# Gate product of a decoder block: weights' split ahead of the gates in each step, the last sum of weights added from SBUF, fewer products on GpSimd

## The chip, the cores and the metric

The kernel runs on one core of a Trainium2 chip, in one launch. The metric is device time in microseconds (us) of that core; the kernel before takes 863.55 us (median of three executions, 863.21 to 864.05). All data are float32. Matrix products are made with three float32r passes: each operand is cut into a rounded part ("hi", by ScalarE) and the rest ("lo", by VectorE), and hi·hi, hi·lo and lo·hi are summed.

## The reference, cut to what matters

Sequence 512, width 1024. A gated convolution and an mLSTM branch are merged into the residual stream `x`; then comes the end of the block, where the change lies:

```python
x = x + jnp.einsum('bsd,de->bse', merged, w_o[l])
gate = jax.nn.sigmoid(jnp.einsum('bsd,de->bse', rmsnorm(x, g_ple[l]), w_ple_gate[l]))
x = x + gate * jnp.einsum('bsp,pd->bsd', p[l], w_ple[l])
return rmsnorm(x, g_final)
```

`p·w_ple` was made early and waits in DRAM (`ple_d`). What is left at the end of the kernel is the gate's product (512 x 1024 by 1024 x 1024), the sigmoid, the gated addition, the sum of squares of each row, and the last scaling.

## The kernel before, in words

The gate's product is done by a Strassen scheme of seven products of half size. Its left operands are 256 rows by 512 (sums of quarters of the transposed `x`), its right operands 512 x 512 quarters of `w_ple_gate` or sums of them. g11, g21, g22, g12 are the four quarters, loaded in that order into four raw buffers. In the order of the program:

| product | left | weights | PSUM bank | what follows each half |
|---|---|---|---|---|
| 0 | g_a11 | g11 | acc | copy out (`snap`) |
| 1 | g_s1 | g11+g12 | cc | copy out |
| 2 | g_a12 | g21 | bb | gate of rows 2 or 3, first half (`g1`) |
| 3 | g_s2 | g11+g12+g22 | acc | copy out |
| 4 | g_s4 | g22 | cc | gate of rows 2 or 3, second half (`g3`) |
| 5 | g_s3 | g12+g22 | acc | gate of rows 0 or 1, second half (`g5`) |
| 6 | g_a22 | all four | acc | gate of rows 0 and 1, first half (`gated`) |

Product n uses operand n. The list `operands` holds, for each, the raw buffer that it is split from and the sums that are made once it has been split: operand 0 is split from g11, which then gets g12 added; operand 1 from the same buffer, which then gets g22; operand 2 from g21, after which g12 gets g22; operand 3 again from g11's buffer (three quarters by now), which then gets g21 and so holds all four for operand 6; operand 4 from g22, operand 5 from g12. The sums are DMAs of GpSimd's queue that add a quarter from DRAM into the raw buffer (line 179), 512 KB for each half.

Each product has two halves `i` of 128 rows, each of 12 matmuls of 128x512 (four `kt` by three passes, L227 to L229); a "row" below is one of the four groups of 128 rows of `x`. Splitting one half of an operand (`split_half`) is one ScalarE instruction (hi, L172, 128x1024) and one VectorE instruction (lo, L173); half 0 holds kt 0 and 1, half 1 kt 2 and 3. Operands 1 to 4 go through two sets of shared buffers (`whi`, `wlo`); the others have tiles of their own: operand 0 `wearly`, 5 `wlate`, 6 `wlast`.

Order is set by hand: no scheduler moves anything on TensorE, VectorE, ScalarE or GpSimd, and each engine runs its instructions strictly in the order in which the program issues them. After each half product the program calls `step`, which calls `tick`. A tick first starts the work that follows the last half product (`fresh`), then splits one half of an operand from the queue `pieces`, then goes on with older work (`active`). `next_operand` empties `pieces` before a product begins and queues the next operand.

After products: `gate` adds two sums (VectorE, L1348) and takes the sigmoid (ScalarE, L1349). `embed` multiplies with `ple` (VectorE, L1295) and adds to `x`, either on VectorE (L1299) or as an adding DMA from SBUF to SBUF by GpSimd's queue (L1297); before, rows 2 and 3 use the DMA. `squares` is a ScalarE instruction (L1302); `add_base`, `power`, `final_scale` are tiny VectorE and GpSimd instructions for the row's factor. `final` writes half a row of output: either VectorE multiplies `x` by the factor and by `g_final` (L1326, stored by SP's queue), or ScalarE scales a product `xg = x * g_final` that GpSimd made earlier (`weigh`, L1334; L1324, stored by ScalarE's queue). Before, GpSimd makes four such products and ScalarE writes four of the eight half rows.

Of the kernel before, what the change touches and what calls it, by code (L numbers as in the profile page):

```python
# [14 lines left out]
P = 128  # L15
# [14 lines left out]
HC = 4  # L30
# [6 lines left out]
def hybrid_block(ctx, tc, x, p, g_mix, w_in, conv_w, conv_b, w_a_out, b_gates, g_head,  # L37
# [87 lines left out]
    for n in range(2):  # L125
# [4 lines left out]
    operands.extend([(g11, [(g11, g12, None)]), (g11, [(g11, g22, None)]), (g21, [(g12, g22, None)]),  # L130
                     (g11, [(g11, g21, None)]), (g22, []), (g12, []), (g11, [])])
# [9 lines left out]
    state = {"raw": 0, "split": 0, "use": 0}  # L141
# [28 lines left out]
    def split_half(i, h, e_lo=None):  # L170
# [1158 lines left out]
    def weigh(t, n):  # L1329

        if not xg:
            u = ep.tile([P, 4, CW], F32, name="xg", tag="fx", align_bytes=256)
            xg.update({key: u[:, i, :] for i, key in enumerate(((3, 0), (3, 1), (0, 1), (1, 1)))})
        pool.tensor_tensor(xg[(t, n)], xr[:, t, half[n]], gfin[:, half[n]], ALU.mult)  # L1334
# [16 lines left out]
    def g1(i):  # L1351
# [9 lines left out]
        if t == 3:  # L1361
            weigh(t, 0)

    def g3(i):
# [4 lines left out]
        embed(c, t, half[1], True)  # L1369
        yield  # L1370
        yield
        yield
        squares(t, half[1], 1)
        power(t, 1)
        if t == 3:
            weigh(t, 1)

    def g5(i):
# [4 lines left out]
        weigh(i, 1)  # L1383
        add_base(i, 0)

    def cut_one():
        if pieces:
            split_half(*pieces.popleft())

    for left, banks, tag, post in ((g_a11, acc, order[0], snap(sn, "s", acc)), (g_s1, cc, order[1], snap(sv, "v", cc)),  # L1390
# [4 lines left out]
        if left is g_s2:  # L1395
            i = early + 5
            own[i] = [glp.tile([P, HC, CW], F32R, name="wlate", tag=f"gl{v}", align_bytes=256) for v in (0, 2)]
            pieces.extend((i, h) for h in range(2))
            u = hp.tile([P, 2, HC, CW], F32R, name="wlast", tag="vv", align_bytes=256)
            last = [u[:, v] for v in range(2)]  # L1400
        for i in range(2):
# [6 lines left out]
            if left is g_s2:  # L1408
# [3 lines left out]
        if left is g_s2:  # L1412
# [69 lines left out]
```

## Time and profile before

| | |
|---|---|
| median of three executions | 863.55 us |
| profiled execution, its own time | 864.67 us |
| its span, first to last instruction | 862.9 us |
| TensorE busy | 844.0 us (98%) |
| VectorE busy | 643.0 us (75%) |
| ScalarE busy | 501.7 us (58%) |
| GpSimd busy | 230.8 us (27%) |
| mean granted TensorE clock | 0.992 |

Times in a trace are us from the span's start. A matmul's row lasts longer than the distance to the next, since matmuls are pipelined; the same holds, less strongly, for VectorE and ScalarE. In brackets behind a row stands how long the engine was idle before it and what ended that. GpSimd's busy time holds its DMA issues.

### The profile page before, as it was taken

How to read it: one execution, taken by the hardware profiler on the slowest of the kernel's cores; microseconds unless marked ns; L12 is line 12 of the kernel's file. 1: busy time of each engine (PE TensorE's matmuls, PEld its weight loads, DVE VectorE, ACT ScalarE, POOL GpSimd, SP SyncE). 2: the span in 40 equal slices, each digit the busy share in tenths (PEclk: the TensorE clock that was granted, in tenths of full speed). 3: DMA queues.
4: the chain of work that ended last, by engine and by line, in shares of the span. 5: the costliest groups of instructions: out<-in, count | busy, mean ns of one | idle time of the engine just before them, and what ended most of it. 6: DMA issues, size and time to landing. Idle time of an engine off the chain costs nothing.

```text
span 862.9 us, 12184 instructions
## 1 busy us (share of the span) xinstructions
PE 844.0 (98%) x4634; PEld 734.1 (85%) x4634; DVE 643.0 (75%) x835; ACT 501.7 (58%) x737; POOL 230.8 (27%) x233
## 2 busy tenths in 40 slices
PE   8999999999999999999999999999999999999983
PEld 7888888888899988888788999999988888888863
DVE  5786767975877675788676879788876789955765
ACT  7467655667755566565776554645452366535654
POOL 5103222203225331320232434242410122111423
PEclk9999999999999999999999999999999999999996
DMA  9749669779968997896997799898995697665844
GB/s 313 263 135 186 156 135 219 183 280 239 257 130 195 247 214 171 188 221 218 246 240 179 188 192 180 177 186 203 169 403 209 100 236 177 206 232 146 196 74 122
DMA packets 102890, 172.82 MB, mean 200 GB/s; under 512 B 5612, under 2 KB 46112, under 8 KB 101552
## 3 DMA queue, kind: packets, MB, share of 16 engines
q0 software_dynamic: 41424, 76.10, 46.3%
q1 hardware_dynamic: 58256, 90.45, 31.6%
q10 hardware_dynamic: 3152, 5.51, 1.8%
q8 instruction: 36, 0.59, 0.3%
q14 instruction: 22, 0.18, 0.1%
HBM read 154.21 MB, written 16.78 MB: 198 GB/s over the span
## 4 chain that ended last, share of the span: by engine, by line
PE 90%; DVE 4%; ACT 3%; issue 1%; DMA 1%; SPq 0%; ACTq 0%; POOL 0%; DVEq 0%
PE mm L227 27%; PE mm L228 27%; PE mm L229 27%; PE pv L227 1%; PE pv L229 1%; PE pv L228 1%; DMA wraw<-in_w_ple 1%; PE pty L809 1%; PE sc L229 1%; PE sc L228 1%; PE sc L227 1%; ACT whi L172 1%; DVE wlo L173 0%; DVE gs L1295 0%; DVE gs L1348 0%
## 5 line engine op out<-in xcount | busy, mean ns | idle before, releaser
L173 DVE TENSOR_TENSOR wlo<-wraw,whi 128x1024 fp32r<-128x1024 f32 x238 | 297.3, 1251 | 120.5 <-ACT whi L172 119.8
L172 ACT ACTIVATE whi<-wraw 128x1024 fp32r<-128x1024 f32 x240 | 250.8, 1054 | 105.9 <-PE mm L229 43.7
L179 POOL DMA_DIRECT2D wraw<-in_w_in x112 | 136.8, 1421 | 317.4 <-DVE wlo L173 236.6
L343 ACT ACTIVATE s<-mm 128x512 f32<-128x512 f32 x84 | 50.2, 597 | 99.1 <-PE mm L229 97.9
L227 PE MATMUL mm<-whi,hs 128*128 128x512 f32 x256 | 99.9, 390 | 0.0
L228 PE MATMUL mm<-wlo,hs 128*128 128x512 f32 x256 | 99.9, 390 | 0.0
L229 PE MATMUL mm<-whi,hs 128*128 128x512 f32 x256 | 99.7, 390 | 0.0
L227 PE MATMUL mm<-hn_hi,whi 128*128 128x256 f32 (+1 forms) x304 | 93.4, 307 | 0.0
L229 PE MATMUL mm<-hn_hi,wlo 128*128 128x256 f32 (+1 forms) x304 | 93.0, 306 | 0.0
L228 PE MATMUL mm<-hn_lo,whi 128*128 128x256 f32 (+1 forms) x304 | 92.9, 306 | 0.0
L227 PE MATMUL mm<-hs,whi 128*128 128x256 f32 x320 | 90.9, 284 | 0.0
L229 PE MATMUL mm<-hs,wlo 128*128 128x256 f32 x320 | 90.6, 283 | 0.0
L228 PE MATMUL mm<-hs,whi 128*128 128x256 f32 x320 | 90.6, 283 | 0.0
L227 PE MATMUL mm<-whi,hn_hi 128*128 128x512 f32 x192 | 75.4, 393 | 0.0
L228 PE MATMUL mm<-wlo,hn_hi 128*128 128x512 f32 x192 | 75.0, 391 | 0.0
L229 PE MATMUL mm<-whi,hn_lo 128*128 128x512 f32 x192 | 74.8, 389 | 0.0
L228 PEld LDWEIGHTS mm<-hs,whi 128*128 128x128 f32 x320 | 61.4, 192 | 0.0
L227 PEld LDWEIGHTS mm<-hs,whi 128*128 128x128 f32 x320 | 61.4, 192 | 0.0
L229 PEld LDWEIGHTS mm<-hs,wlo 128*128 128x128 f32 x320 | 61.4, 192 | 0.0
L229 PEld LDWEIGHTS mm<-hn_hi,wlo 128*128 128x128 f32 x304 | 58.1, 191 | 2.5
L228 PEld LDWEIGHTS mm<-hn_lo,whi 128*128 128x128 f32 x304 | 58.1, 191 | 2.4
L227 PEld LDWEIGHTS mm<-hn_hi,whi 128*128 128x128 f32 x304 | 58.1, 191 | 2.4
(362 smaller groups left out, 1718.6 us busy)
## 6 DMA issues: line engine op xcount, KB each, us to landing
wraw<-in_w_in SPq DMA_DIRECT2D x32, 1024.0 KB, 5.4
wraw<-in_w_in POOLq DMA_DIRECT2D x52, 512.0 KB, 7.9
wraw<-in_w_in SPq DMA_DIRECT2D x48, 512.0 KB, 5.2
wraw<-in_w_in POOLq DMA_DIRECT2D x60, 256.0 KB, 6.0
wraw<-in_w_b_out SPq DMA_DIRECT2D x7, 1024.0 KB, 6.2
wraw<-in_w_b_out POOLq DMA_DIRECT2D x12, 512.0 KB, 6.5
yt_d<-yc POOLq DMA_DIRECT2D x4, 1024.0 KB, 4.9
wraw<-in_w_a_out SPq DMA_DIRECT2D x4, 1024.0 KB, 5.8
```

What stands on the lines that cost most here:

```text
L172: act.activation(hi, t, AF.Copy)
L173: (e_lo or dve).tensor_tensor(lo, t, hi.bitcast(F32), ALU.subtract)
L179: nc.gpsimd.dma_start(raws[to][:, ks, cs], src[:, ks, :], accum_op=ALU.add)
L227: pe.matmul(ps, lhsT=a[0], rhs=b[0], start=first, stop=False, **kw)
L228: pe.matmul(ps, lhsT=a[0], rhs=b[1], start=False, stop=False, **kw)
L229: pe.matmul(ps, lhsT=a[1], rhs=b[0], start=False, stop=last, **kw)
L343: act.activation(to[i], src, AF.Copy, scale=scale)
L809: pe.transpose(pts[v][:, t * P:(t + 1) * P], y[:, t, v * P:(v + 1) * P], ident)
```

## The change

1. In the gate's product a tick splits a half operand first and starts the gates afterwards (`weights_first`).
2. Operand 5 (`wlate`) is split in the steps of product 1 (before: product 3), and operand 6 (`wlast`) in the steps of product 2 (before: product 4). Product 2's steps now split operand 3's two halves and `wlast`'s two. Their tiles change places to what is free at that time.
3. The sum of all four quarters is made in g21 instead of g11: when operand 2 has been split from g21, a DMA of GpSimd's queue adds the raw g11 (three quarters by then) from SBUF into g21. That replaces the two DRAM additions behind operand 3.
4. `embed` of rows 2 and 3, second half, adds on VectorE instead of by DMA.
5. GpSimd makes two products `xg` instead of four; row 3's output is made by VectorE and stored by SP. The order of the last instructions is changed accordingly.

```diff
-    operands.extend([(g11, [(g11, g12, None)]), (g11, [(g11, g22, None)]), (g21, [(g12, g22, None)]),
-                     (g11, [(g11, g21, None)]), (g22, []), (g12, []), (g11, [])])
+    operands.extend([(g11, [(g11, g12, None)]), (g11, [(g11, g22, None)]), (g21, [(g12, g22, None), (g21, g11, "here")]),
+                     (g11, []), (g22, []), (g12, []), (g21, [])])
...
+            if eng == "here":
+                nc.gpsimd.dma_start(raws[to][:, ks, :], raws[c][:, ks, :], accum_op=ALU.add)
+                continue
...
     def tick():
+        if state["weights_first"]:
+            cut_one()
         new = [g for g in fresh if not next(g, True)]
         fresh.clear()
-        if pieces:
-            split_half(*pieces.popleft())
+        if not state["weights_first"]:
+            cut_one()
         active[:] = [g for g in active if not next(g, True)] + new
...
     def g3(i):
         t = 2 + i
         c = sn[i]
         gate(c, cc[i], t, ner)
         yield
-        embed(c, t, half[1], True)
-        yield
-        yield
-        yield
+        embed(c, t, half[1])
         squares(t, half[1], 1)
+        yield
         power(t, 1)
-        if t == 3:
-            weigh(t, 1)
...
-        if left is g_s2:
-            i = early + 5
-            own[i] = [glp.tile([P, HC, CW], F32R, name="wlate", tag=f"gl{v}", align_bytes=256) for v in (0, 2)]
-            pieces.extend((i, h) for h in range(2))
-            u = hp.tile([P, 2, HC, CW], F32R, name="wlast", tag="vv", align_bytes=256)
-            last = [u[:, v] for v in range(2)]
+        if left is g_s1:
+            u = hp.tile([P, 2, HC, CW], F32R, name="wlate", tag="vv", align_bytes=256)
+            place(early + 5, u[:, 0], u[:, 1])
+        if left is g_a12:
+            place(early + 6, *[glp.tile([P, HC, CW], F32R, name="wlast", tag=f"gl{v}", align_bytes=256) for v in (0, 2)])
...
             step(post(i))
-            if left is g_s2:
+            if left is g_a12:
                 cut_one()
...
+    final(2, 1)
     gated(1, 1)
     squares(0, q[1], 2)
     power(0, 2)
-    final(2, 1)
+    final_scale(3)
+    final(3, 0)
     squares(1, q[1], 2)
     power(1, 2)
-    final_scale(3)
-    final(3, 0, True)
-    final(3, 1, True)
+    final(3, 1)
     final_scale(0)
     final(0, 1, True)
     final(0, 0)
```

Three places show what this does to the order. In these rows the raw buffers are wraw_7091 (g11), wraw_7170 (g21), wraw_7278 (g22) and wraw_7342 (g12), and the lines of the changed kernel are 9 higher from L200 on.

First, GpSimd's queue around products 0 and 1, before:

```order
L179 DMA wraw_7091<-in_w_ple_gate 128x2x512 x4
L179 DMA wraw_7342<-in_w_ple_gate 128x2x512 x2
L1165 DMA ple<-ple_d 128x1024 x4
L1257 TENSOR_TENSOR etmp_7118<-etmp_7117,mhalf 128x4
L179 DMA wraw_7091<-in_w_ple_gate 128x2x512 x2
```

and in the changed kernel:

```order
L182 DMA wraw_7091<-in_w_ple_gate 128x2x512 x4
L182 DMA wraw_7342<-in_w_ple_gate 128x2x512
L177 DMA wraw_7170<-wraw_7091 128x1024
L182 DMA wraw_7342<-in_w_ple_gate 128x2x512
L177 DMA wraw_7170<-wraw_7091 128x1024
L1174 DMA ple<-ple_d 128x1024 x4
L1266 TENSOR_TENSOR etmp_7118<-etmp_7117,mhalf 128x4
```

The second addition into g12 now stands behind the first addition from SBUF, and the loads of `ple` and the power of L1257 (now L1266) behind the second one.

Second, ScalarE from the first copy of product 0's sums to the operand of product 4, before (gf: quarter of the transposed `x`; glb: left operands g_a12 and g_s4; gs: copies and gates):

```order
L1342 ACTIVATE gs<-mm 128x512
L1195 ACTIVATE gf_7533<-ptk,prm 128x256 x2
L1195 ACTIVATE gf_7534<-ptk,prm 128x256 x2
L234 ACTIVATE glb<-gf_7533 128x512
L234 ACTIVATE glb<-gf_7534 128x512
L1342 ACTIVATE gs<-mm 128x512 x2
L172 ACTIVATE whi_7613<-wraw_7091 128x1024
L234 ACTIVATE glb<-fx 128x1024
L1349 ACTIVATE gs<-gs,er 128x512
L172 ACTIVATE whi_7635<-wraw_7091 128x1024
L1349 ACTIVATE gs<-gs,er 128x512
L172 ACTIVATE whi_7657<-wraw_7278 128x1024
```

and the later part of the same stretch in the changed kernel:

```order
L172 ACTIVATE wlate<-wraw_7342 128x1024
L1351 ACTIVATE gs<-mm 128x512
L172 ACTIVATE whi_7620<-wraw_7091 128x1024
L1351 ACTIVATE gs<-mm 128x512
L243 ACTIVATE glb<-fx 128x1024
L172 ACTIVATE whi_7628<-wraw_7091 128x1024
L172 ACTIVATE wlast<-wraw_7170 128x1024
L1358 ACTIVATE gs<-gs,er 128x512
L172 ACTIVATE wlast<-wraw_7170 128x1024
L172 ACTIVATE whi_7663<-wraw_7278 128x1024
L1358 ACTIVATE gs<-gs,er 128x512
L172 ACTIVATE whi_7683<-wraw_7278 128x1024
```

The second half of `wlate` stands ahead of operand 3's first half, both halves of `wlast` ahead of operand 4's first half, and a gate's sigmoid between each pair. (The first half of `wlate` stands one copy earlier, ahead of L1195's rows.)

Third, VectorE over the same products, before:

```order
L1236 TENSOR_TENSOR fx<-fx,gf_7534 128x512
L173 TENSOR_TENSOR wlo_7614<-wraw_7091,whi_7613 128x1024
L235 TENSOR_TENSOR glb<-fx,glb 128x1024
L1348 TENSOR_TENSOR gs<-gs,mmb 128x512
L173 TENSOR_TENSOR wlo_7636<-wraw_7091,whi_7635 128x1024
L1348 TENSOR_TENSOR gs<-gs,mmb 128x512
L173 TENSOR_TENSOR wlo_7658<-wraw_7278,whi_7657 128x1024
L1295 TENSOR_TENSOR gs<-gs,ple 128x512
L173 TENSOR_TENSOR wlo_7664<-wraw_7278,whi_7663 128x1024
```

and in the changed kernel:

```order
L1245 TENSOR_TENSOR fx<-fx,gf_7536 128x512
L173 TENSOR_TENSOR wlo_7621<-wraw_7091,whi_7620 128x1024
L244 TENSOR_TENSOR glb<-fx,glb 128x1024
L173 TENSOR_TENSOR wlo_7629<-wraw_7091,whi_7628 128x1024
L173 TENSOR_TENSOR wlast<-wraw_7170,wlast 128x1024
L1357 TENSOR_TENSOR gs<-gs,mmb 128x512
L173 TENSOR_TENSOR wlast<-wraw_7170,wlast 128x1024
L173 TENSOR_TENSOR wlo_7664<-wraw_7278,whi_7663 128x1024
L1357 TENSOR_TENSOR gs<-gs,mmb 128x512
L1304 TENSOR_TENSOR gs<-gs,ple 128x512
L173 TENSOR_TENSOR wlo_7684<-wraw_7278,whi_7683 128x1024
```

Operand 3's second half (wlo_7629) now precedes the first gate instead of following it, and the two halves of `wlast` precede operand 4's (wlo_7664, wlo_7684).

More of the change, by code (lines that the diff above doesn't have):

```diff
@@ L140, in hybrid_block @@
                 last_use[c] = i
-    state = {"raw": 0, "split": 0, "use": 0}
+    state = {"raw": 0, "split": 0, "use": 0, "weights_first": False}
     raws, splits, pieces, active, fresh = {}, {}, deque(), [], []
@@ L189, in queue_split @@
         i = state["split"]
-        if i in own:
+        while i in own:
             i += 1
@@ L194, in queue_split, with cut_one @@
             pieces.extend((i, h) for h in range(2))
+    def cut_one():
+        if pieces:
+            split_half(*pieces.popleft())
     def next_operand(follow=True):
@@ L1327, in final, with weigh @@
         (nc.scalar if on_act else nc.sync).dma_start(out[0, t * P:(t + 1) * P, half[n]], y)
-    def weigh(t, n):
+    def weigh(t):
         if not xg:
-            u = ep.tile([P, 4, CW], F32, name="xg", tag="fx", align_bytes=256)
-            xg.update({key: u[:, i, :] for i, key in enumerate(((3, 0), (3, 1), (0, 1), (1, 1)))})
-        pool.tensor_tensor(xg[(t, n)], xr[:, t, half[n]], gfin[:, half[n]], ALU.mult)
+            u = ep.tile([P, 2, CW], F32, name="xg", tag="fx", align_bytes=256)
+            xg.update({(t, 1): u[:, t, :] for t in range(2)})
+        pool.tensor_tensor(xg[(t, 1)], xr[:, t, half[1]], gfin[:, half[1]], ALU.mult)
     acc, bb, cc, sn, sv = ([None, None] for _ in range(5))
@@ L1360, in g1 @@
         add_base(t, 0)
-        if t == 3:
-            weigh(t, 0)
     def g3(i):
@@ L1368, in g3 @@
         yield
-        embed(c, t, half[1], True)
+        embed(c, t, half[1])
+        squares(t, half[1], 1)
         yield
-        yield
-        yield
-        squares(t, half[1], 1)
         power(t, 1)
-        if t == 3:
-            weigh(t, 1)
     def g5(i):
@@ L1382, in g5, with place @@
         squares(i, half[1], 0)
-        weigh(i, 1)
+        weigh(i)
         add_base(i, 0)
-    def cut_one():
-        if pieces:
-            split_half(*pieces.popleft())
+    def place(i, *tiles):
+        own[i] = list(tiles)
+        pieces.extend((i, h) for h in range(2))
+    state["weights_first"] = True
     for left, banks, tag, post in ((g_a11, acc, order[0], snap(sn, "s", acc)), (g_s1, cc, order[1], snap(sv, "v", cc)),
@@ L1411, in hybrid_block @@
             load_ple()
-        if left is g_s2:
-            own[early + 6] = last
     w = next_operand()
```

## The prediction

> **What bounds the kernel now.** I read the stages of the end first (us of the stage, then busy time and instructions of TensorE, its weight loads, VectorE, ScalarE and GpSimd, granted clock, DMA share, GB/s):
>
> ```profile
> 820.78:827.25 6.47, 5.76 (x25) 4.42 (x24) 3.53 (x4) 4.58 (x7) 1.21 (x1) 1.00 0.76 117
> 827.25:832.69 5.44, 5.44 (x25) 4.50 (x24) 5.44 (x7) 3.02 (x4) 1.74 (x2) 1.00 0.74 128
> 832.69:840.43 7.74, 5.60 (x25) 4.35 (x24) 4.60 (x8) 3.73 (x8) 1.49 (x2) 1.00 0.09 16
> 840.43:847.10 6.67, 3.10 (x25) 2.90 (x25) 4.18 (x10) 3.87 (x10) 4.87 (x5) 0.91 0.46 79
> 847.10:852.60 5.50, 5.49 (x24) 5.19 (x24) 4.94 (x13) 2.30 (x8) 2.09 (x3) 0.50 0.07 26
> 852.60:862.90 10.30, 0.00 (x0) 0.00 (x0) 4.59 (x16) 4.26 (x9) 1.50 (x2) 0.67 0.51 190
> ```
>
> The first two are products 3 and 4, the third product 5 and the wait behind it, the next two product 6, the last has no matmul. An undisturbed product takes 5.44 us. Then the order of time on TensorE from 803 on shows its only waits:
>
> ```profile
> 823.26 0.50 PE L228 MATMUL mm<-wlo,gl 128*128 128x512 f32 x1 [0.71 <-DVE wlo L173]
> 840.43 0.36 PE L227 MATMUL mm<-wlast,gl 128*128 128x256 f32 x1 [2.14 <-DVE gs L1348]
> 847.10 0.58 PE L227 MATMUL mm<-wlast,gl 128*128 128x256 f32 x1 [3.56 <-ACT eq L1425]
> ```
>
> So some 6.4 us of waits and a last stage of 10.3 us are open to the change; before 803 the two programs are the same. VectorE and ScalarE set all of it: each runs in order and they pass results to and fro.
>
> **How I cost it.** I took the changed order of the five queues and set each instruction at the later of two times: when its engine is free, and when its inputs are there, with durations of the rows below. Consecutive 1.22 us instructions of VectorE start 1.14 apart (821.98 to 823.12 below), 0.68 us ones 0.60 apart, ScalarE's 1.05 us ones 0.95.
>
> ```profile
> 805.53 1.22 DVE L1223 TENSOR_TENSOR fx<-fx 128x1024 f32<-128x1024 f32 x1
> 809.09 1.23 DVE L173 TENSOR_TENSOR wlo<-wraw,whi 128x1024 fp32r<-128x1024 f32 x1 [1.74 <-ACT whi L172]
> 815.14 0.15 DVE L242 TENSOR_TENSOR etmp<-etmp,etmp 128x4 f32<-128x4 f32 x1
> 816.00 1.28 DVE L1236 TENSOR_TENSOR fx<-fx,gf 128x512 f32<-128x512 f32 x2
> 817.21 1.22 DVE L173 TENSOR_TENSOR wlo<-wraw,whi 128x1024 fp32r<-128x1024 f32 x1
> 818.42 1.23 DVE L235 TENSOR_TENSOR glb<-fx,glb 128x1024 fp32r<-128x1024 f32 x1
> 821.98 1.23 DVE L173 TENSOR_TENSOR wlo<-wraw,whi 128x1024 fp32r<-128x1024 f32 x1 [1.74 <-ACT whi L172]
> 823.12 0.68 DVE L1348 TENSOR_TENSOR gs<-gs,mmb 128x512 f32<-128x512 f32 x1
> ...
> 834.86 2.02 DVE L173 TENSOR_TENSOR wlast<-wraw,wlast 128x1024 fp32r<-128x1024 f32 x1 [1.74 <-ACT wlast L172]
> 841.40 0.68 DVE L1295 TENSOR_TENSOR gs<-gs,ple 128x512 f32<-128x512 f32 x1
> 842.12 0.69 DVE L1299 TENSOR_TENSOR xr<-xr,gs 128x512 f32<-128x512 f32 x1
> 843.66 0.15 DVE L1311 TENSOR_SCALAR base<-fss 128x1 f32<-128x1 f32 x1 [0.85 <-ACT fsq L1302]
> ```
> ```profile
> 813.24 1.17 ACT L234 ACTIVATE glb<-gf 128x512 fp32r<-128x512 f32 x2
> ...
> 817.32 1.07 ACT L234 ACTIVATE glb<-fx 128x1024 fp32r<-128x1024 f32 x1 [0.23 <-DVE fx L1236]
> 823.84 0.73 ACT L1349 ACTIVATE gs<-gs,er 128x512 f32<-128x512 f32 x1 [1.89 <-DVE gs L1348]
> 826.84 2.00 ACT L172 ACTIVATE wlate<-wraw 128x1024 fp32r<-128x1024 f32 x2
> 842.90 0.63 ACT L1302 ACTIVATE fsq<-xr 128x512 f32<-128x512 f32 x1 [0.66 <-DVE xr L1299]
> 846.59 0.46 ACT L1425 ACTIVATE eq<-mm,er 128x256 f32<-128x256 f32 x1
> 852.63 0.47 ACT L1425 ACTIVATE eq<-mm,er 128x256 f32<-128x256 f32 x1 [1.69 <-PE mm L229]
> 859.76 0.34 ACTq L1327 DMA_DIRECT2D out<-y  x1
> ```
>
> GpSimd's queue and its DMAs (the `x1` row is the landing of the last of the four additions of 798.91):
>
> ```profile
> 798.91 4.91 POOL L179 DMA_DIRECT2D wraw<-in_w_ple_gate  x4 [15.16 <-DVE wlo L173]
> 809.70 2.18 POOL L1165 DMA_DIRECT2D ple<-ple_d  x4 [5.88 <-issue]
> 823.52 1.21 POOL L179 DMA_DIRECT2D wraw<-in_w_ple_gate  x1 [3.52 <-DVE wlo L173]
> 834.50 1.29 POOL L1334 TENSOR_TENSOR xg<-xr,gfin 128x512 f32<-128x512 f32 x1 [3.11 <-DMA xr<-gs]
> ...
> wraw<-in_w_ple_gate POOLq DMA_DIRECT2D x1, 512.0 KB, 11.5
> ```
> ```profile
> 801.50 2.32 POOL L179 DMA_DIRECT2D wraw<-in_w_ple_gate  x1
> ```
> ```profile
> DMA to landing us min/median/max: 3.3/3.6/3.9
> ```
>
> **The change part by part.**
>
> (a) *Addition from SBUF.* In the row of four, the last two are the additions into g12; the last was issued at 801.50 and landed 11.5 later, 813.0. Now the second of them stands behind an addition from SBUF that must wait until VectorE has split operand 2's first half. That split now follows L1223 (free at 806.7): 806.7 to 807.9 instead of 809.1. GpSimd starts 0.3 after its releaser (VectorE's 821.98 + 1.23 = 823.21, issue 823.52), so the SBUF addition is issued at 808.2, takes 1.2, and g12's second half follows at 809.4, 7.9 later than before. When does it land? An addition of 512 KB from SBUF is not in the trace. The nearest row, 256 KB from SBUF (`xr<-gs`, the landing line), takes 3.3 to 3.9; one of 512 KB from DRAM alone 5.7:
>
> ```profile
> wraw<-in_w_ple_gate POOLq DMA_DIRECT2D x1, 512.0 KB, 5.7
> ```
>
> From 3.9 to, by doubling, 7.8; I take 5.2, between the two rows, and 2.9 for each further one in the queue (four issued 0.7 apart end with the last at 11.5, against 5.6 for the first: (11.5 + 2.6 − 5.6) / 3 = 2.8). Thus 813.4 for the first, 816.05 for g12's second half.
>
> (b) *`wlate` into product 1.* ScalarE, with the first half of `wlate` (0.95) and the second copy-out ahead of the quarter's copies, ends its L234 pair at 815.6 instead of 814.4; VectorE's part of them comes 0.6 later, and product 2, due at 820.78 − 5.44 = 815.34, loses 0.3. Then it waits for g12 until 816.15, 0.55 us, and splits: to 817.2. VectorE: `wlate` to 818.4, five small ones (815.14 to 816.00: 0.86), two L1236 (1.2), operand 3's first half 820.5 to 821.7. Product 3, due at 821.1, waits 0.7. L235, released by ScalarE at 821.7, ends at 822.95, operand 3's second half at 824.1; TensorE has done 6 matmuls of 0.227 by 823.1 and waits 1.0 again. Product 3 ends at 828.1, 0.85 late; the old wait of 0.7 is in that.
>
> (c) *`wlast` into product 2.* VectorE: first half of `wlast` to 825.2, first gate to 825.8. ScalarE: sigmoid 0.7, second half of `wlast`, operand 4's first half, to 828.5. VectorE: `wlast` 827.6, operand 4's first half 828.8 to 830.0, second gate to 830.6; ScalarE: sigmoid, operand 4's second half to 832.3; VectorE to 833.6. So product 4 has its second kt pair at 833.7, and 17 matmuls of 0.227 later ends at 837.55, against 832.69: **4.9 us late**. This is the largest term: four halves that ran under products 3 to 5 now stand ahead of operand 4, and TensorE waits.
>
> (d) *From the last gate of product 4 to product 6's second part.* Product 5 has its weights, and product 6 as well. But now VectorE makes product 4's last gate (837.7 to 838.4), ScalarE its sigmoid and squares (to 839.9), and then come four rounds of multiply, add, squares, for rows 2, 3, 0 and 1, each waited for by the next small instruction of VectorE. One round is 841.40 to 843.66 in the rows above, 2.26, and 0.1 for the small one: 840.0, 842.4, 844.75, 847.1. The gates of product 5 fall into the waits. The fourth has 0.35 of slowing beside an `xg` product (834.86 shows 2.02 instead of 1.22 beside GpSimd's 834.50): its squares end at 849.8, and `eq` starts behind them at 849.6 against 846.59: **+3.0**. The two gains that the edit has here, the old 2.14 wait gone (product 5's first gate is read long before) and 1.9 of the lateness caught up, are in that difference. Part 4 (two L1299 on VectorE, 1.2 us, for two DMAs of 3.3) lies in these rounds.
>
> (e) *The end.* TensorE has been idle for over 3 us, as before, and runs product 6's second part at half rate as before: from `eq` to the last `eq` 6.04 before (846.59 to 852.63), 5.9 now; last `eq` 855.5. From there to the last store's issue it was 7.13 (852.63 to 859.76), with four ScalarE outputs 1.15 apart. Now ScalarE has two, VectorE four more between the rows' factors: embed 856.0 to 856.9, factor of row 0 and the two outputs of row 3 to 858.8, row 0 to 860.0, row 1's factor 860.6, output and issue 861.4: 5.9. **−1.2 to −1.3**. So the store goes out at 861.4 against 859.76, **+1.7**.
>
> (f) *Clock.* In the stage 840.43:847.10 the mean is 0.91: 1.2 us at half rate, so it fell at 845.9, 2.4 us after TensorE's last matmul, while the 2.14 us wait left it at 1.00. Between 828.6 and 833.7 TensorE now works about a third of the time in two bursts. Below: nothing; above: matmuls at double length through the rest of product 4, which moves (d) by 17 × 0.227 × 0.44 = 1.7. I take half of it, 0.85, since the two rows lie on either side.
>
> The Trainium skill (TensorE: Matmul & The Clock Gate, Part 1: The HAM clock gate) says that the clock is halved after an idle window of some 3.4 us on a grid that does not start with the kernel. By that rule the broken run of product 4 costs nothing and the sum stays at +1.7; the trace agrees only in part, since 2.4 idle us sufficed. It also says (DMA: Bandwidth & Descriptors, Anatomy of one DMA — SWDGE (gpsimd) path) that such a DMA takes 2.0 us plus its bytes at 436 GB/s, by estimate 3.2 for 512 KB; then the wait of 0.55 in (b) vanishes and the sum is +1.2. The trace's 5.7 speaks against it.
>
> Sum: +3.0 − 1.3 + 0.85 = +2.55. The profiled execution's 864.67 (span 862.9 and 1.8 around it) becomes 867.2; the median shown lies 1.1 lower, so 863.55 + 2.55 = **866.1**. With an addition from SBUF of 3.9 the sum without clock is +1.0 (ScalarE's wait gone, 0.55, and VectorE's next 0.2), with 7.8 it is +4.4, as the 0.55 wait grows by 2.6; its own range is 864.5 to 868.8.
>
> **The rivals.** *No measurable change* (0.2%, 1.7 us, is what a measurement here can tell). A short addition and no loss of clock: 863.55 + 1.0 = 864.6. For it: the 3.3 us rows. Against: g12's first half fills the queue until about 810 (813.0 − 2.9), so a faster DMA gains little.
>
> *Faster.* Product 4's weights come in time, because the split that leads each tick wins back what the extra halves cost. Then product 4 ends near 832.7 as before, (d)'s 12 us from gate to `eq` end at 844.7, 1.9 before the old 846.59, and (e) adds 1.2: −3.1, 860.4. It decides at operand 4's second half: it must be split by 829 (827.25, six matmuls and a little). For it: VectorE has 2.9 us free of 6.5 in product 3's stage. Against: five splits and two gates stand in one chain there, 2 us for each hand-over.
>
> *Slower still.* The addition takes 7.8: 863.55 + 4.4 = 868.0. For it: it reads both operands from SBUF, and 256 KB needs over half the time of 512 KB from DRAM. Against: what is fixed in the 3.3 isn't doubled.
>
> **How the numbers follow.** Forecast 0.47, no change 0.25, faster 0.12, slower still 0.16. Forecast and slower still are both slower by over 0.2%: 0.63. I give the range 862.8 to 868.6, which leaves out the faster case and the last part of the slowest.
>
> **What would show it.** After: TensorE waits for L173 (`wlo`) twice in product 3 and for ScalarE and VectorE four times in product 4, some 5 us; no wait of 2 us ahead of product 6; `wlate`'s second half on ScalarE starts at 816, released by a DMA; the wait for `eq` is 3 to 4 us; the last store is issued 5.9 after the last `eq`. Wrong if product 4 ends before 834, or if `eq` starts before 846.6.

## The result, and the profile after

| | before | after |
|---|---|---|
| median | 863.66 us (6 executions) | 867.9 us (6 executions) |
| lowest, highest | 863.21, 864.25 | 866.0, 869.4 |
| profiled execution | 864.67 us | 868.92 us |
| its span | 862.9 us | 867.1 us |

The changed kernel is slower: after over before is 1.0047, 95% interval 1.0032 to 1.0062, or +4.1 us. The prediction said 866.1 with +2.55; the direction and the place were right, the median is 1.8 us above the forecast.

In the profiled execution of the changed kernel everything ahead of the change comes 0.24 us later than in that of before: the last VectorE row that the change doesn't touch (L1223 of before, `fx`, at 805.53) starts at 805.77. The row doesn't depend on the change, and over all runs below it starts anywhere from 804.93 to 806.70, so the 0.24 is no more than chance. In what follows this row is the **anchor**, and times are compared from it.

The order of time on TensorE after, only the rows with a wait:

```profile
822.56 0.50 PE L237 MATMUL mm<-wlo,gl 128*128 128x512 f32 x1 [0.98 <-DVE wlo L173]
...
824.90 0.50 PE L237 MATMUL mm<-wlo,gl 128*128 128x512 f32 x1 [0.68 <-DVE wlo L173]
...
829.29 0.49 PE L236 MATMUL mm<-whi,glb 128*128 128x512 f32 x1 [0.25 <-ACT whi L172]
...
830.74 0.50 PE L237 MATMUL mm<-wlo,glb 128*128 128x512 f32 x1 [0.95 <-DVE wlo L173]
...
833.04 0.49 PE L236 MATMUL mm<-whi,glb 128*128 128x512 f32 x1 [0.87 <-ACT whi L172]
...
834.30 0.50 PE L237 MATMUL mm<-wlo,glb 128*128 128x512 f32 x1 [0.76 <-DVE wlo L173]
...
839.90 0.40 PE L236 MATMUL mm<-wlate,gl 128*128 128x512 f32 x1
...
852.37 0.51 PE L236 MATMUL mm<-wlast,gl 128*128 128x256 f32 x1 [3.96 <-ACT eq L1426]
```

Before there was one wait in product 3 (0.71), none in product 4, and 2.14 ahead of product 6. Now two stand in product 3 and four in product 4 (2.83 us together by the brackets), and the 2.14 is gone. The row at 839.90 is the first of product 5: product 4 ends there, 839.90 − 805.77 = 34.13 behind the anchor against 832.69 − 805.53 = 27.16 before, so **7.0 us late**, where the prediction had 4.9 and, with its share of the clock, some 5.7. The stages (product 3, product 4, product 5, product 6's first part with the wait behind it, its second part, the rest; columns as in the prediction):

```profile
821.10:829.04 7.94, 6.27 (x26) 4.21 (x24) 6.20 (x7) 5.37 (x6) 0.00 (x0) 1.00 0.37 148
829.04:839.90 10.86, 8.03 (x24) 5.70 (x25) 5.51 (x8) 4.17 (x8) 1.80 (x2) 0.84 0.29 50
839.90:845.36 5.46, 5.46 (x25) 4.50 (x24) 3.55 (x7) 2.67 (x6) 0.47 (x1) 1.00 0.00 0
845.36:852.37 7.01, 3.05 (x26) 2.84 (x24) 4.77 (x10) 3.20 (x9) 3.76 (x4) 1.00 0.00 0
852.37:857.40 5.03, 4.63 (x24) 4.42 (x24) 4.49 (x13) 2.06 (x7) 0.12 (x1) 0.66 0.14 52
857.40:867.10 9.70, 0.00 (x0) 0.00 (x0) 5.39 (x18) 2.46 (x7) 1.52 (x2) 0.60 0.51 189
```

Product 4 takes 10.86 us instead of 5.44, and its clock is 0.84. The brackets count from the end of a row, which lasts 0.39 us where the next could start after 0.227; counted from there, the four waits take 3.7 us. From 834.30, where its last wait ends, 17 matmuls were left: 17 × 0.227 = 3.85 us, but product 5 begins 5.60 later. These 1.75 us are lost to the clock, but for some 0.1 by which the row at 834.30 is slow after its wait.

ScalarE after, the rows that the prediction named:

```profile
816.98 1.06 ACT L172 ACTIVATE wlate<-wraw 128x1024 fp32r<-128x1024 f32 x1 [1.19 <-DMA wraw<-in_w_ple_gate]
...
851.86 0.82 ACT L1426 ACTIVATE eq<-mm,er 128x256 f32<-128x256 f32 x2
...
857.04 0.47 ACT L1426 ACTIVATE eq<-mm,er 128x256 f32<-128x256 f32 x1 [0.90 <-PE mm L238]
...
863.28 0.36 ACTq L1336 DMA_DIRECT2D out<-y  x1
```

The first `eq` is 46.09 behind the anchor, before 41.06: **+5.03**. From it to the end of the span it takes 15.24 us, before 862.9 − 846.59 = 16.31: **−1.07**. The sum, 3.96, and the 0.24 ahead of the anchor are the 4.20 between the two spans (4.25 between the times of the two executions).

The four rounds of VectorE are there one behind the other, 2.33, 2.40, 2.38 and 2.69 us apart (VectorE after; each row waits for ScalarE's squares, the last round holds an L1304 of 1.04 instead of 0.68):

```profile
842.19 0.15 DVE L1320 TENSOR_SCALAR base<-fss 128x1 f32<-128x1 f32 x1 [1.40 <-ACT fsq L1311]
...
844.52 0.22 DVE L1315 TENSOR_SCALAR etmp<-fss,base 128x1 f32<-128x1 f32 x1 [0.25 <-ACT fsq L1311]
...
846.92 0.21 DVE L1315 TENSOR_SCALAR etmp<-fss,base 128x1 f32<-128x1 f32 x1 [0.26 <-ACT fsq L1311]
...
849.30 0.15 DVE L1320 TENSOR_SCALAR base<-fss 128x1 f32<-128x1 f32 x1 [0.85 <-ACT fsq L1311]
849.37 1.04 DVE L1304 TENSOR_TENSOR gs<-gs,ple 128x512 f32<-128x512 f32 x1
...
851.99 0.15 DVE L1320 TENSOR_SCALAR base<-fss 128x1 f32<-128x1 f32 x1 [0.85 <-ACT fsq L1311]
```

### The profile page after: what moved, and what is told of

The parts are those of the page before. It is cut to its first block, busy times and chain, and to the rows that moved or that the text cites. A ratio compares the mean times of both kernels' runs of the same rounds, so it can differ in the third digit from the quotient of the medians.

```text
span 867.1 us, 12181 instructions
## 1 busy us (share of the span) xinstructions
PE 846.2 (98%) x4634; PEld 733.8 (85%) x4634; DVE 644.6 (74%) x839; ACT 500.5 (58%) x735; POOL 226.3 (26%) x229
## 4 chain that ended last, share of the span: by engine, by line
PE 88%; DVE 5%; DMA 2%; ACT 2%; issue 2%; SPq 0%; POOL 0%; ACTq 0%; DVEq 0%
PE mm L236 27%; PE mm L237 27%; PE mm L238 27%; PE pv L236 1%; DVE wlo L173 1%; PE pv L237 1%; PE pv L238 1%; DMA wraw<-in_w_ple_gate 1%; PE pty L818 1%; DMA wraw<-in_w_b_out 1%; DMA xin<-in_x 1%; PE sc L238 1%; PE sc L237 1%; PE sc L236 1%; PE pt L555 0%
```

## The experiments

My theory after the result: the prediction's chain is right (weights split too early, then rounds that follow each other), and the missing part is the clock in product 4. Rivals: the addition from SBUF sets it all off; the order in a tick costs; the clock is hidden behind VectorE. Every kernel was timed beside runs of the kernel before on its chip; ratios are to that. "eq" and "end" are the first `eq` and the end of the span, counted from the anchor in the profiled execution.

| kernel | median us | ratio, 95% interval | eq | end |
|---|---|---|---|---|
| before | 863.7 to 864.1 | 1 | 41.06 | 57.37 |
| after | 867.9 | 1.0047 (1.0032, 1.0062) | 46.09 | 61.33 |
| 1 part 5 alone | 862.73 | 0.9987 (0.9977, 0.9996) | 40.22 | 55.38 |
| 2 after, `wlast` late | 865.84 | 1.0018 (1.0009, 1.0027) | 42.66 | 58.85 |
| 3 after, clock held | 866.57 | 1.0031 (1.0019, 1.0042) | 44.44 | 59.09 |
| 4 part 5, `eq` early | 862.99 | 0.9985 (0.9976, 0.9994) | 37.23 | 55.47 |
| 5 parts 4 and 5 | 865.28 | 1.0016 (1.0007, 1.0025) | 42.19 | 57.50 |
| 6 after, both late | 866.39 | 1.0028 (1.0017, 1.0039) | 43.22 | 59.32 |
| 7 after without part 1 | 869.66 | 1.0073 (1.0060, 1.0086) | 47.16 | 62.45 |
| 8 after, SBUF additions last | 866.97 | 1.0035 (1.0022, 1.0047) | 44.77 | 59.92 |
| 9 as 3, part 4 undone | 865.75 | 1.0023 (1.0013, 1.0033) | 43.75 | 58.61 |
| 10 part 5, clock held | 862.29 | 0.9985 (0.9976, 0.9994) | 40.22 | 55.04 |
| 11 what is left, clock held | 862.26 | 0.9983 (0.9975, 0.9992) | 40.38 | 55.28 |
| 12 as 11, row 2 earlier | 861.90 | 0.9977 (0.9967, 0.9987) | 40.31 | 54.76 |

The profiled executions of before and of after each took 1.0 us more than their medians, with anchors (805.53, 805.77) in the middle of the range, so "end" stands up to that much too high in the first two rows. Against each other the two compare fairly. Where another row is compared with one of them, part of the difference can be this, and the ratio has the last word.

### 1. Part 5 alone

Against before, with `weigh` as in the change:

```diff
-        if t == 3:
-            weigh(t, 0)
...
+    final(2, 1)
     gated(1, 1)
...
-    final(3, 0, True)
-    final(3, 1, True)
+    final(3, 0)
...
+    final(3, 1)
```

> The kernel before with part 5 of the change alone: two products xg on GpSimd instead of four, row 3's two output halves made by VectorE and stored by SP, the new order of the last instructions. Theory (term (e)): the last stage loses 1.2 to 1.3 us, nothing ahead of it moves: ratio to the kernel before 0.9985, 862.3 us; VectorE's wlast split no longer takes 2.02 us where GpSimd made a product. Rival: VectorE is the full engine of the end, and its four more products cost what ScalarE saves: ratio 1.000 to 1.002.

Measured: 0.9987, −1.1 us. Term (e) was priced −1.2 to −1.3, and its own stretch agrees: from first `eq` to the end it takes 861.3 − 846.14 = 15.16 us, as in the changed kernel (15.24), against 16.31 before. But the expectation that nothing ahead of it moves doesn't hold in the traces: `eq` comes 0.84 earlier too, since VectorE's second split of `wlast` takes 1.23 us where it took 2.02 beside GpSimd's `xg` (VectorE of this kernel):

```profile
835.24 1.23 DVE L173 TENSOR_TENSOR wlast<-wraw,wlast 128x1024 fp32r<-128x1024 f32 x1 [1.74 <-ACT wlast L172]
```

Together that is 2.0 us in the traces and 1.1 in the ratio. Whether before's other executions have the slow split isn't shown; its profiled one is 1.0 us above the median.

### 2. `wlast` split where it was before

```diff
-        while i in own:
+        if i in own:
...
-        if left is g_a12:
-            place(early + 6, *[glp.tile([P, HC, CW], F32R, name="wlast", tag=f"gl{v}", align_bytes=256) for v in (0, 2)])
...
+        if left is g_s2:
+            own[early + 6] = [glp.tile([P, HC, CW], F32R, name="wlast", tag=f"gl{v}", align_bytes=256) for v in (0, 2)]
```

> The changed kernel with operand 6 (wlast) split where it was before, in the steps of product 4 (its tiles kept); wlate stays in product 1, the addition from SBUF and the order in a tick stay. Theory (term (c), the largest): without wlast's two halves ahead of operand 4, product 4's waits shrink from 2.8 us to under 1 and the clock is not cut in it: 2 to 2.5 us faster than the changed kernel, ratio to the kernel before 1.001 to 1.0025, 864.5 to 865.7 us. Rival (the addition from SBUF is what costs, by the 1.2 us ScalarE waits for it and all that queues behind): the time stays within 0.5 us of the changed kernel, ratio 1.0045, 867.5 us. Rival (the order in a tick costs, as gates come later): also unchanged.

Measured: 1.0018, 2.5 us less than after. The waits of product 4 that stay are these (TensorE):

```profile
830.01 0.49 PE L236 MATMUL mm<-whi,glb 128*128 128x512 f32 x1 [0.32 <-ACT whi L172]
...
831.27 0.50 PE L237 MATMUL mm<-wlo,glb 128*128 128x512 f32 x1 [0.77 <-DVE wlo L173]
```

1.09 us instead of 2.83, the clock stays at 1.00 to 845, and `eq` comes 3.4 us earlier; 0.9 of that is lost again at the end, where product 6's second part now runs at half rate throughout. The largest term, (c), is the one named.

### 3. The clock held

Matmuls into a PSUM tile that nobody reads, in the waits of product 4 and ahead of product 6's second part:

```diff
+    def busy(n):
+        if not idle:
+            idle.append(ps_x.tile([P, S], F32, name="idle", tag="x"))
+        for _ in range(n):
+            pe.matmul(idle[0], lhsT=g_a12[0][:, 0, :P], rhs=own[early + 5][0][:, 0, :], start=True, stop=True)
...
+                if left is g_s4 and i == 0 and kt == 2:
+                    busy(4)
...
     gated(0, 0)
+    busy(15)
     last_part(0, 1)
```

and `busy(5)` behind the first matmul of kt 0 and 2 in product 4's first half.

> The changed kernel with matmuls added whose results nothing reads: 14 of 128x512 in the waits of product 4's first half, 15 ahead of product 6's second part. They change no order on any other engine. Theory (term (f) as the trace of the changed kernel shows it: half rate from 835.4 to 838.8 and again in product 6's second part): the clock stays at 1.00 to the end of the matmuls, product 5 and product 6's second part run at full rate; 2.5 to 3.5 us faster than the changed kernel, ratio to the kernel before 1.000 to 1.002, 864.0 to 865.4 us, and its executions spread by 1 us instead of 3. Rival (waits alone set the time and the clock's loss is hidden behind VectorE and ScalarE): no gain, 867.5 to 868.5 us, ratio 1.0045 to 1.0055.

Measured: 1.0031, 1.4 us less than after, and the executions spread by 1.2 us instead of 3.3. The two intervals overlap, so the size rests on the traces. Here are the stretch from shortly ahead of product 4 into product 5 (cut at 836) and product 6's second part:

```profile
828.20:836.00 7.80, 7.56 (x32) 5.49 (x31) 5.47 (x7) 3.64 (x6) 1.80 (x2) 1.00 0.21 36
836.00:841.40 5.40, 5.40 (x26) 4.46 (x25) 2.19 (x5) 2.67 (x6) 0.00 (x0) 1.00 0.28 49
850.86:854.50 3.64, 3.12 (x24) 2.92 (x24) 3.43 (x11) 2.18 (x7) 0.13 (x1) 1.00 0.00 0
```

The clock is 1.00, `eq` comes 1.65 us earlier, and from `eq` to the end it takes 14.65 instead of 15.24. So in the profiled executions the clock in product 4 reaches `eq` nearly whole (1.75 lost there, 1.65 got back); in product 6's second part TensorE gains 1.4 (3.64 against 5.03) and the end 0.6, because VectorE is nearly full there (3.43 of 3.64). I expected 2.5 to 3.5 and it gave 1.4 by the medians and 2.2 in the traces, where after stands up to 1.0 too high: the expectation had passed on too much of the last stage. The rival without gain had 867.5 or more, and all six executions lie below that.

### 4. `eq` earlier

```diff
     last_part(1, 0)
-    tick()
     gated(0, 0)
     last_part(0, 1)
+    tick()
     drain()
```

on the kernel of experiment 1.

> As the kernel with part 5 alone, but in the step before the last the gated addition of row 0, the one that frees the bank for product 6's second part (eq), is issued ahead of the first gates' remaining work of the tick. Theory: the wait for eq in product 6 (3.56 us before) is set by where eq stands on ScalarE, not by its inputs; eq moves up by 1 to 1.5 us and the end with it: 1.0 to 1.3 us faster than part 5 alone, ratio to the kernel before 0.997, 861.0 us. Rival: eq waits for VectorE's rounds of multiply, add and squares wherever it is issued: same as part 5 alone, ratio 0.9985.

Measured: 0.9985 against 0.9987, no difference. `eq` did move, by 3 us, and the wait for it fell to 0.50 us; the last stage only grew as long. The theory that the first `eq` bounds the end falls. What the edit did was to move the wait: row 1's round of multiply, add and squares now stands behind the first `eq`, the second `eq` comes 41.62 behind the anchor (41.19 in experiment 1), and TensorE waits for that one instead:

```profile
847.05 0.39 PE L227 MATMUL mm<-wlast,gl 128*128 128x256 f32 x1 [2.69 <-ACT eq L1421]
```

So this says nothing of a kernel in which both come earlier. That VectorE's list sets the end from there on is read from the trace (VectorE has no wait from 847.03 to 856.5), not shown by this run.

### 5. Parts 4 and 5

```diff
-        embed(c, t, half[1], True)
-        yield
-        yield
-        yield
+        embed(c, t, half[1])
         squares(t, half[1], 1)
+        yield
         power(t, 1)
```

on the kernel of experiment 1.

> The kernel before with parts 4 and 5 of the change: rows 2 and 3 add their second half on VectorE instead of by DMA, and the end is the new one. Weights, addition and order in a tick are those of before. Theory (term (d)): the two additions and the waits for their squares make four rounds of VectorE and ScalarE of 2.4 us out of two, one behind the other, so eq comes 1.0 to 1.4 us later than with part 5 alone although nothing ahead of product 5 changes: ratio to the kernel before 1.0000 to 1.0005, 864.1 to 864.5 us. Rival: VectorE has room there and the 3.3 us of the two DMAs go: as fast as part 5 alone or faster, ratio 0.9987 or less.

Measured: 1.0016, 2.5 us more than part 5 alone; in the traces `eq` comes 1.97 later and the end 2.12. The theory had 1.0 to 1.4: right in kind, too small. In experiment 1 the additions of rows 2 and 3 are DMAs that GpSimd issues, and VectorE goes on; with part 4 VectorE goes through four rounds that each end in a wait for squares, not two (VectorE of this kernel, then of experiment 1):

```profile
841.62 0.21 DVE L1306 TENSOR_SCALAR etmp<-fss,base 128x1 f32<-128x1 f32 x1 [0.25 <-ACT fsq L1302]
...
844.01 0.21 DVE L1306 TENSOR_SCALAR etmp<-fss,base 128x1 f32<-128x1 f32 x1 [0.25 <-ACT fsq L1302]
...
846.40 0.15 DVE L1311 TENSOR_SCALAR base<-fss 128x1 f32<-128x1 f32 x1 [0.85 <-ACT fsq L1302]
...
849.02 0.15 DVE L1311 TENSOR_SCALAR base<-fss 128x1 f32<-128x1 f32 x1 [0.85 <-ACT fsq L1302]
```
```profile
843.25 0.15 DVE L1311 TENSOR_SCALAR base<-fss 128x1 f32<-128x1 f32 x1 [0.85 <-ACT fsq L1302]
...
846.26 0.15 DVE L1311 TENSOR_SCALAR base<-fss 128x1 f32<-128x1 f32 x1 [0.85 <-ACT fsq L1302]
```

From the first multiply (L1295) to the row ahead of the first `eq` it is 839.37 to 849.02 here and 838.60 to 846.26 there, 9.65 against 7.66. So part 4, of two instructions and 1.2 us, costs 2.0 (traces) to 2.5 us (ratios) by itself; the rows put it down to ScalarE's squares, which VectorE waits for between the rounds.

### 6. Both operands late

```diff
-        if left is g_s1:
+        if left is g_s2:
             u = hp.tile([P, 2, HC, CW], F32R, name="wlate", tag="vv", align_bytes=256)
...
-            if left is g_a12:
+            if left is g_s2:
                 cut_one()
```

and `wlast` as in experiment 2. The last line moves the step's second split from product 2 to product 3, where `wlate`'s halves are again.

> The changed kernel with wlate and wlast both split where they were before (steps of products 3 and 4); the order in a tick, the addition from SBUF, parts 4 and 5 stay. Theory: TensorE's waits in products 3 and 4 shrink to under 1.5 us together, no clock cut there; what is left over the kernel with parts 4 and 5 is the gates' later start, 0.5 to 1.5 us: ratio to the kernel before 1.0005 to 1.002, 864.5 to 865.8 us, not better than with wlast back alone by more than 0.5. Rival (wlate in product 1, with its wait for g12, costs by itself): 1 us or more faster than with wlast back alone, ratio 1.0005 or less.

Measured: 1.0028, not better than `wlast` late alone (1.0018). So `wlate` in product 1, with its wait for g12, isn't what costs; the rival is out. Against parts 4 and 5 alone (1.0016) parts 1 and 3 are left, +1.0 us by the ratios with overlapping intervals; in the traces `eq` comes 1.03 later.

### 7. Without part 1

```diff
-    state["weights_first"] = True
```

> The changed kernel without part 1: in a tick the gates are started first and the split follows, as before. Theory: part 1 is what keeps operands 3 and 4 from coming later still; without it each half of them stands behind one more gate's round trip, product 4's waits grow by 2 us or more: ratio to the kernel before 1.006 to 1.009, 869.5 to 872 us. Rival: splits first delay the gates that product 5 and the end need; without part 1 the time falls by 1 us, ratio 1.0035.

Measured: 1.0073, 2.2 us more; the intervals just touch, but all five executions (869.4 to 871.1) lie above the six of after. Part 1 is a gain in this change, not a cost. The place was expected wrongly: product 4's waits don't grow, they shrink from 2.83 to 1.90 us. TensorE's waits grow in product 3 (2.54 us for `wlo`, where it was 0.98), and its clock is 0.50 from 823.2 to 830.0:

```profile
824.33 0.80 PE L237 MATMUL mm<-wlo,gl 128*128 128x512 f32 x1 [2.54 <-DVE wlo L173]
```

### 8. SBUF additions behind the DRAM ones

```diff
-                nc.gpsimd.dma_start(raws[to][:, ks, :], raws[c][:, ks, :], accum_op=ALU.add)
+                for hs_ in (slice(0, HH), slice(HH, HC)) if h == 1 else ():
+                    nc.gpsimd.dma_start(raws[to][:, hs_, :], raws[c][:, hs_, :], accum_op=ALU.add)
```

> The changed kernel with the first addition from SBUF issued together with the second, so that g12's second addition stands ahead of both in GpSimd's queue. Theory (term (a)): g12's second half lands 2.5 to 3 us earlier (before 814), ScalarE's 1.2 us wait ahead of wlate's second half goes; of that 0.4 to 0.7 us reaches the end, since VectorE's chain to operand 4 takes the rest: ratio to the kernel before 1.0035 to 1.0045, 867.2 to 868 us. Rival: that wait is the first step of the whole delay and its going takes 1.2 us or more from the time: ratio 1.003 or less. Rival: the additions from SBUF land so much later that wlast's halves now wait for them: no gain, ratio 1.005.

Measured: 1.0035, 1.0 us less than after, with wide overlap; in the traces, where after stands up to 1.0 too high, `eq` comes 1.32 earlier. ScalarE splits `wlate`'s second half at 815.15 without a wait for a DMA. The time from issue to landing of the first addition from SBUF after, the DRAM addition behind it and the second addition from SBUF, then of both additions from SBUF in this kernel (last number, us):

```profile
wraw<-wraw POOLq DMA_DIRECT2D x1, 512.0 KB, 4.9
wraw<-in_w_ple_gate POOLq DMA_DIRECT2D x1, 512.0 KB, 8.0
...
wraw<-wraw POOLq DMA_DIRECT2D x1, 512.0 KB, 6.3
```
```profile
wraw<-wraw POOLq DMA_DIRECT2D x1, 512.0 KB, 7.1
...
wraw<-wraw POOLq DMA_DIRECT2D x1, 512.0 KB, 5.6
```

The theory's 0.4 to 0.7 and the rival's 1.2 lie on either side of the 1.0, and the overlap leaves both open. If the size is right, the wait is about a quarter of the 4.1 us.

### 9. Part 4 undone in the changed kernel, clock held

The diff of experiment 5 reversed, on the kernel of experiment 3.

> The changed kernel with part 4 undone (rows 2 and 3 add their second half by DMA again), and with the added matmuls whose results nothing reads, so that the clock stays up as in the kernel with the clock held. Theory: part 4's two rounds of VectorE and ScalarE stand in the chain to eq here too, as in the kernel before, where they took 2.1 to 2.5 us; the DMAs cost little in their place: 1.5 to 2.5 us faster than the changed kernel with the clock held, ratio to the kernel before 1.000 to 1.0015, 863.8 to 865.1 us. Rival: here product 4 ends late, so the two DMAs of 3.3 us, issued after its last gate, become the end of the chain and give most of it back: 0.7 us or less faster, ratio 1.0022 to 1.0031.

Measured: 1.0023, 0.7 us less than experiment 3: the rival's number (the two intervals overlap; in the traces `eq` comes 0.69 earlier). Its reason is wrong, though. VectorE's gate of row 1 waits for TensorE, not for a DMA:

```profile
844.30 0.69 DVE L1359 TENSOR_TENSOR gs<-gs,mm 128x512 f32<-128x512 f32 x1 [1.40 <-PE mm L240]
```

Product 5 ends late because product 4 did, and this is next in line once the rounds are gone. The two delays lie beside each other: part 4 costs 2.5 us alone and some 0.7 behind a late product 4.

### 10. Part 5, clock held

`busy(14)` ahead of `last_part(0, 1)` in experiment 1's kernel.

> The kernel before with part 5, and 14 matmuls of 128x512 whose results nothing reads in the wait ahead of product 6's second part. Theory: that part runs at full rate, its last eq comes 1.3 us earlier after the first; VectorE, which is full from there on, passes 0.6 us of it on: 0.5 to 0.8 us faster than part 5 alone, ratio to the kernel before 0.9978 to 0.9982, 861.9 to 862.3 us. Rival: the last stage is VectorE's alone and the clock is worth nothing there: ratio 0.9987.

Measured: 0.9985 against 0.9987, not told apart; in the traces the end comes 0.34 earlier. The clock in the last part is worth 0.3 (here) to 0.6 us (experiment 3) in the traces, less than the ratios can tell.

### 11. What is left of the change, clock held

The changed kernel with the diffs of experiments 2 and 8, part 4 undone, and `busy(14)` as in 10.

> The changed kernel without what has cost time so far: part 4 undone, wlast split in product 4 as before, both additions from SBUF issued together; parts 1 and 5 and wlate in product 1 stay, and the 14 added matmuls hold the clock ahead of product 6's second part. Theory: what is left of parts 1 to 3 neither gains nor costs more than 0.5 us: ratio to the kernel before 0.997 to 0.9985, 861.3 to 862.5 us, within 0.5 us of the kernel before with part 5 and the clock held. Rival: the addition from SBUF and wlate's early split cost 1 us by themselves (as parts 1 and 3 seemed to, 1.0028 against 1.0016): ratio 0.999 or more.

Measured: 0.9983, the same as experiment 10. What stays of parts 1 to 3 neither gains nor costs as far as the ratios can tell; part 5 is what gains.

### 12. Row 2's first output earlier

```diff
         weigh(i)
+        if i:
+            final_scale(2)
+            final(2, 0)
         add_base(i, 0)
```

on the kernel of experiment 11, with the two lines taken out further down.

> The changed kernel with part 4 undone, wlast split in product 4, both additions from SBUF issued together and the clock held ahead of product 6's second part, and in addition row 2's factor and its first output half are made before the wait of VectorE for row 1's squares (0.85 us idle there), not after the first eq. Theory: from the first eq on VectorE has no idle time, so the 1.27 us taken out of that stretch come off the end, less 0.4 to 0.6 by which they overrun the wait and are slowed beside GpSimd's product: 0.6 to 0.9 us faster than the same kernel without it, ratio to the kernel before 0.9973 to 0.9977. Rival: the end is set by the chain from the last eq through squares and power to the row's factor, and VectorE's earlier outputs only fill gaps in it: no gain, ratio 0.9983.

Measured: 0.9977, the fastest median (861.90), but its interval holds 0.9983 too; the end comes 0.52 earlier in the trace, where 0.6 to 0.9 was expected. Part of the gain goes where a one-column instruction of VectorE takes 1.02 us instead of 0.16 beside GpSimd's `xg` (845.21, 1.28 us):

```profile
845.48 1.02 DVE L1327 TENSOR_TENSOR fs<-etmp,etmp 128x1 f32<-128x1 f32 x1
```

Experiments 1, 4 and 10 to 12 beat both kernels, by 0.1 to 0.2%; so the good part of the change is part 5.

## Why the prediction was right, and what it sized wrong

**(a) Addition from SBUF: right, a little short.** First addition 5.2 predicted, 4.9 measured; the second took 6.3. But the DRAM addition behind the first came 8.0 us after its issue at 808.99, at 816.98; the prediction had 816.05 + 0.24 = 816.3. The spacing in the queue was 3.7 us, not 2.9. By the prediction's own terms, 813.4 + 2.9, it would have been 816.3 + 0.24, so a third of the difference is a slip in its sum (and the four additions of before are issued 0.86 apart, 2.6 over three, not 0.7). So ScalarE waited 1.19 instead of 0.55. The Trainium skill's fit (DMA: Bandwidth & Descriptors, Anatomy of one DMA — SWDGE (gpsimd) path), 3.2 us for 512 KB by estimate, doesn't agree with 4.9 and 6.3 here; the measurement decides.

**(b) Product 3: right.** Waits of 0.7 and 1.0 predicted, 0.98 and 0.68 found, and product 4 began at 829.04 where 828.1 + 0.24 was predicted, 0.7 later: the wait for the DMA is 0.64 longer than predicted.

**(c) Product 4: right.** Operand 4's second half ended at 834.24 against 833.6 + 0.24 predicted. Four waits, as said, but not "some 5" us: 2.83 by the brackets, 3.7 counted from where the next matmul could start. The 4.9 is how late product 4 ends, and 0.85 of it is product 3's, so that the prediction's own terms have 4.0 for the waits. Experiment 2 shows that `wlast` is behind 2.5 of the 4.1 us.

**(d) The rounds: right.** 2.4 us each, and `eq` 5.03 late where the sum had 3.0 without and 3.85 with its share of the clock. Experiments 5 and 9 show how it is put together: part 4's two rounds and the late product 4 lie beside each other, so neither can be added to the other.

**(e) The end: right in sum, by luck in part.** −1.2 to −1.3 predicted, −1.07 in the trace, −1.15 in experiment 1's (its own times, 5.9 and 5.9 against 6.04 and 7.13, come to −1.37). It came about differently, and three deviations cancel: product 6's second part got its clock back at 855.88 and took 5.18 us instead of 5.9 from first to last `eq`; from there to the last store's issue it was 6.24 instead of 5.9, and from that to the end of the span 3.8 instead of the 3.1 of before.

**(f) The clock: mis-sized for the profiled execution; for the median that isn't shown.** The prediction took 0.85, half of its upper bound of 1.7. No row gives the factor 0.44 in that bound; at double length all 17 matmuls would lose 3.9. That the bound comes near the loss is luck: the half rate lasted 3.4 us and held about 8 of the 17. The loss was 1.75 in product 4, and 1.65 of it reached `eq` (experiment 3). In the profiled executions the account closes: 867.2 predicted, 868.92 measured, 1.7 more; of these 0.9 are the clock (1.75 for 0.85), 0.4 what is left of the late DMA at operand 4's second half, 0.24 lie ahead of the anchor and 0.2 at the end.

The median needs another account. The six executions of the changed kernel differ with their mean clock: 866.0 and 866.4 us at 0.993 and 0.994, 867.8 to 869.4 at 0.991 and 0.992, so not every one loses 1.75. By the medians holding the clock gained 1.4 us, and with 0.3 to 0.6 of that in the last stage (experiments 10 and 3) some 0.8 to 1.1 are left for product 4, about what was predicted. Then most of the 1.8 us by which the median lies above the forecast is something else. A likely part is the base: the prediction was worked out from an execution of before that took 1.0 us more than its median, and carried the whole difference over to the median. No run shows this.

The rivals: "faster" needed operand 4's second half by 829; it came at 834.24. "No change" needed no loss of clock. "Slower still" gave 868.0, the measured median, but by luck: the addition from SBUF took 4.9, not 7.8.

What stays open: what the median's excess over the forecast consists of, and what parts 1 and 3 alone cost over the kernel with parts 4 and 5 (1.0 us by the ratios, the intervals overlap).

## What to carry to other kernels

An operand that is made ready earlier pushes back what stands behind it on an engine that works in order; count the instructions ahead of the next operand that is needed, not the average load of the engine (`wlast`: 2.5 us). Work moved from a DMA to an engine can cost not its own time, but the round trip between the engines that wait for each other (here 1.2 us of work, 2.0 to 2.5 us). Short gaps in matmuls can cost twice, once as a wait and once as clock (3.7 and 1.75 us in product 4 of the profiled execution). Two late chains that run side by side show little until both are mended. And compare a profiled execution with its own median before a difference to it is taken over to medians.

## What the runs showed of the hardware that I had not expected

The clock falls after a stretch in which TensorE works only part of the time, without any long gap. After, in pieces of 3.41 us laid on the fall at 835.40 (TensorE's busy time is the first number behind the comma, the clock the third from the right):

```profile
828.57:831.98 3.41, 2.20 (x9) 1.09 (x7) 3.31 (x4) 1.33 (x3) 0.00 (x0) 1.00 0.00 0
831.98:835.40 3.42, 1.79 (x7) 1.11 (x7) 1.82 (x2) 1.98 (x4) 1.18 (x2) 1.00 0.45 77
835.40:838.82 3.42, 3.42 (x10) 2.68 (x9) 0.84 (x2) 1.33 (x3) 0.62 (x1) 0.50 0.49 81
838.82:842.23 3.41, 3.41 (x17) 2.78 (x16) 0.72 (x2) 1.34 (x3) 0.00 (x0) 1.00 0.00 0
...
849.06:852.47 3.41, 0.10 (x1) 0.10 (x1) 2.08 (x5) 1.45 (x6) 2.06 (x2) 1.00 0.00 0
852.47:855.88 3.41, 3.41 (x16) 3.41 (x17) 2.91 (x10) 1.33 (x5) 0.02 (x1) 0.50 0.00 0
```

and before, laid on the fall at 845.93:

```profile
839.10:842.52 3.42, 2.09 (x17) 2.12 (x18) 3.38 (x6) 1.45 (x2) 1.15 (x2) 1.00 0.28 49
842.52:845.93 3.41, 1.01 (x9) 0.81 (x7) 1.95 (x5) 1.40 (x4) 2.77 (x3) 1.00 0.62 105
845.93:849.34 3.41, 2.24 (x10) 2.24 (x11) 2.35 (x8) 2.56 (x8) 2.44 (x3) 0.50 0.00 0
849.34:852.75 3.41, 3.25 (x16) 2.95 (x14) 2.77 (x7) 0.99 (x4) 0.80 (x1) 0.50 0.16 61
```

Each piece is wholly at 1.00 or at 0.50, and the first of a run of pieces at half rate stands behind one with little work: here after busy times of 0.10, 1.01 and 1.79, while after 2.09 and 2.20 the clock stayed. No single gap in the piece with 1.79 was longer than 1.0 us. Busy time as the profile counts it is not the measure, though. In experiment 5 a piece of 1.69 kept the clock, and the next, of 1.11, lost it:

```profile
843.68:847.10 3.42, 1.69 (x12) 1.49 (x12) 2.28 (x6) 1.64 (x5) 2.19 (x2) 1.00 0.00 0
847.10:850.51 3.41, 1.11 (x9) 1.11 (x10) 2.29 (x6) 1.60 (x5) 1.27 (x1) 1.00 0.00 0
850.51:853.93 3.42, 3.42 (x17) 3.22 (x16) 3.25 (x11) 1.23 (x5) 0.00 (x0) 0.50 0.16 62
```

Pieces of 1.60 (experiment 4) and 1.62 (experiment 6) kept it as well. A matmul's row lasts 0.39 to 0.5 us where the next could start 0.227 later, so a few scattered matmuls look like more work than they are. If each counts for its distance to the next at full rate (0.227 us for 512 columns, 0.120 for 256), the piece with 1.79 holds 1.22 and the one with 1.69 holds 1.44. Laid on the falls in before, after and experiments 1, 2 and 4 to 8, the pieces at full rate then sort: all with up to 1.32 us of 3.41 were followed by half rate, all from 1.34 on by full rate. That is an estimate made from these traces afterwards, with no run that tested it. Coming back up took more: pieces at half rate with busy times of 2.24 (before) and 2.51 (experiment 2) were followed by another one, a piece of 2.90 (experiment 8) by full rate.

The Trainium skill (TensorE: Matmul & The Clock Gate, Part 1: The HAM clock gate) has the grid of some 3.4 us and the two rates, and the trace agrees with both; but it speaks of an idle window, and here a window that held 1.22 us of matmuls and no gap over 1.0 us sufficed, so the rows decide. The prediction leaned toward that reading when it halved the term.

An engine's short instruction pays for a neighbour: a one-column instruction of VectorE took 1.02 instead of 0.16 us beside a product of GpSimd (experiment 12) and ended with it, at 846.50 and 846.49; in after a 128x512 one took 1.04 instead of 0.68 beside GpSimd's `xg` (848.60, 1.27 us).
